# Decoder step on one core: sums of weight blocks formed by paced transfers, seven products in the down projection's middle groups, and the low-rank gate stage on quarters of the array

## The chip, the cores and the metric

One Trainium2 chip, one of its cores. The metric is the device time of one execution in microseconds. TensorE (PE) multiplies; VectorE (DVE), ScalarE (ACT) and GpSimd (POOL) work on tiles in SBUF and PSUM; SyncE (SP) here only issues transfers (DMAs). Each engine runs its own queue of instructions in order, and semaphores tie the queues together.

## The reference, cut to what matters

One layer of a decoder for 512 prompt tokens and 64 sample tokens (8 sequences of 8), 1024 channels. Weights are shared.

```
mk, mv = rmsnorm(mem) @ w_xk, rmsnorm(mem) @ w_xv
z = rmsnorm(x) @ w_in        # GLA q,k,v,r, low-rank gate (16 columns), retention q,k,v,g, two merge gates
log_alpha = log_sigmoid(ga_low @ w_gla_a2 + b) / 16        # forget gate of the GLA branch
o_g, o_r = chunked linear attention with decays, per head, with states
merged = sigmoid(gate_a) * norm(o_g) * silu(gr) + sigmoid(gate_b) * norm(o_r) * silu(rg)
x = x + rmsnorm(merged @ w_mix_out)
x = x + rmsnorm(cross_attention(rmsnorm(x)))               # 4 heads, 256 memory tokens
x = x + rmsnorm(square(relu(rmsnorm(x) @ w_up)) @ w_down)  # 4096 hidden
```

## The kernel before

Activations lie channel by token: 576 columns, in two halves of 288 (`NH`), each half 256 prompt and 32 sample tokens. Every float32 operand of a product is split into a high and a low part (`split`, L92 to L94: ACT casts the high part, DVE subtracts to get the low part; `split_p`, L98, has POOL subtract). A product is then three matmuls, high by high, high by low, low by high (`mm3`, L251 to L253). `gemm_m` makes one output block of 128 columns: 8 steps of the inner dimension by three matmuls by two halves, 48 matmuls.

Weights come in tiles of 128 x 1024, 512 KB each, in the order of the list `plan`. `wfetch` (L180) issues the load from SP into one of six raw tiles `wraw`, `wsplit` splits it into `wh` and `wl`, `wnext` hands it to a product.

The stages: keys and values of the memory (`mem`), with the norms of x beside them (`prenorm`, L363, whose low parts `xl` POOL subtracts; `rstd`, L333, takes the power -1/2 on POOL, `dg`, L335, spreads it into a diagonal on DVE, and PE makes it a row by L342). Then the mixers: first the low-rank gate stage, then eight units, each one head of retention or of GLA. In a unit POOL computes the rotary sum (L890), the scaled keys `ks` (L1063), the power of each head's norm (L874), gates `G` (L1127) and merges (L1136). Then the output projection, cross-attention, and the MLP in four groups g of 1024 hidden channels: up, relu squared, down into the sum `y3`.

The gate stage (L806 to L809) takes a weight `w_ga` of 128 columns that holds the 16 columns three times, runs `gemm_m(xh, xl)` on it and leaves in `ga` the high, the low and again the high part, at partitions 0, 32 and 64. `decays` (L833) multiplies it for each GLA head.

`sevenfold` (L281) does the up products of g=1, 2, 3 in 2 x 2 blocks, by channel halves and token halves: seven products of 12 matmuls in place of eight. It needs four sums and differences of weight blocks, which DVE forms in `begin` (L213) from the two loaded tiles, and of activation blocks (`fsh`, `fsl`; A11, A12, A22, S1 to S4 are their names). The split sums lie in `wh`, `wl` and in `wq`. A block is one set of four such quarters of outputs; a group has four blocks. The up products of g=0 and all down products are plain; for g=3 the last norm is joined to them.

The program is written in order, and a scheduler then places each engine's instructions, so that independent work may stand earlier or later than it is written.

Of the kernel before, what the change touches and what calls it, by code (L numbers as in the profile page):

```python
# [13 lines left out]
P = 128  # L14
KT = 8
# [11 lines left out]


RING, STAY, RAW, SEVEN = 0, 1, 2, 3
# [29 lines left out]
def decoder_step(ctx, tc, xT, memT, ktc, vc, s_gla, s_ret, w_in, w_ga, w_a2, w_mix, w_xq, w_xk, w_xv, w_xo,  # L59
                 w_up, w_ups, w_down, vecs, cst, gam, y_out, mk_out, mv_out, sg_p, sr_p, sg_s, sr_s):  # L60
# [15 lines left out]
    ident, ones = idn[:, 0:128], idn[:, 128:256]  # L76
    def f32(ap):
        return ap.bitcast(F32)
# [60 lines left out]
    plan += [w_ga[:, 0]]  # L139
# [23 lines left out]
    def seven(w, b0):  # L163
        return [(w[b0 + b][:, kh], SEVEN) for b in range(4) for kh in range(2)]
# [6 lines left out]
    wq = []  # L171
    units = []

    def wfetch():
        if plan and sum(m == SEVEN for _, m in raws) < 2:
            src, mode = plan.pop(0), RING
            if isinstance(src, tuple):
                src, mode = src
            raw = wp.tile([P, 1024], F32, name="wraw", bufs=N_RAW)
            nc.sync.dma_start(out=raw if len(src.shape) == 2 else raw.rearrange("p (k n) -> p k n", n=src.shape[2]), in_=src)  # L180
            raws.append((raw, mode))

    def wsplit():
        if units:
            units.pop(0)()
        elif raws:
            if raws[0][1] == SEVEN:
                begin()
                return
# [4 lines left out]
            pool = staying[-1] if mode == STAY else wp  # L194
            wh = pool.tile([P, 1024], F32R, name="wh")
            wl = pool.tile([P, 1024], F32R, name="wl")
            split(wh, wl, raw)
            ready.append((wh, wl))

    def halves(w):  # L200
        return w.rearrange("p (q n) -> p q n", q=2)

    def begin():


        while len(raws) < 2:
            wfetch()
        p0, p1 = (raws.pop(0)[0] for _ in range(2))
        t = wp.tile([P, 1024], F32, name="wraw", bufs=N_RAW)
        q0, q1, qt = halves(p0), halves(p1), halves(t)  # L210

        def minus(out, a, b):
            nc.vector.tensor_tensor(out=out, in0=a, in1=b, op=ALU.subtract)  # L213

        def ring(raw):
            wh = wp.tile([P, 1024], F32R, name="wh")
            wl = wp.tile([P, 1024], F32R, name="wl")
            split(wh, wl, raw)
            ready.append((wh, wl))

        def own(raw, o, n):
            w = wq[0][:, o:o + n], wq[0][:, o + n:o + 2 * n]
            split(*w, raw)
            ready.append(w)

        def unit_a():
            ring(p0)
            wfetch()

        units.extend([unit_a, lambda: ring(t), lambda: own(p1, 0, 1024),  # L230
                      lambda: minus(q1[:, 0], q1[:, 0], qt[:, 0]), lambda: own(q1[:, 0], 2048, 512)])
        minus(qt[:, 1], q1[:, 1], q0[:, 1])
        minus(q0[:, 1], q0[:, 1], q0[:, 0])
        minus(qt[:, 0], q1[:, 1], q0[:, 1])
        wfetch()

    def wnext(n=P):

        while sum(len(r) == 2 for r in ready) < 2 and (raws or plan):
            while not units and plan and len(raws) + sum(len(r) == 1 for r in ready) < N_RAW - 1:  # L240
                n0 = len(raws)
                wfetch()
                if len(raws) == n0:
                    break
            if not raws and not units:
# [25 lines left out]


    def sevenfold(x, p1, p5, u2, c11, c22, c12, c21):


# [9 lines left out]
        def more():  # L285
            if units:
# [1135 lines left out]
```

## Time and profile before

| | us |
|---|---|
| median of three runs (lowest, highest) | 1200.71 (1199.32, 1202.62) |
| profiled execution | 1199.37 |
| its span | 1197.6 |
| PE busy in the span | 1168.7 |
| DVE busy | 746.6 |
| ACT busy | 563.3 |
| POOL busy | 155.1 |

A row of the timeline gives start, duration, engine, line, operation, the tile written and the tiles read, and in brackets how long the engine stood idle before it and what ended that. Matmuls overlap in the pipeline: one of 288 columns is listed with about 0.3 us while the next starts 0.13 us later. The memory's keys and values take the span to about 67 us, the gate stage follows, then the mixers; the up products of g=1 lie from 892 to 937 us, its down products from there to 988.

### The profile page before, as it was taken

The numbers are of one execution on the slowest core, as the hardware profiler recorded it, in microseconds if no ns is written. First come the engines' busy times: TensorE is split into PE (matmuls) and PEld (weight loads), VectorE is DVE, ScalarE is ACT, GpSimd is POOL, SyncE is SP. The second block draws the span as 40 slices with busy tenths as digits, with TensorE's granted clock in tenths as the row PEclk, the third lists the DMA queues.
The fourth block names the chain that finished last, engine by engine and source line by source line (L and its number), as shares of the span: only waits on it lengthen the run. The fifth ranks groups of instructions, "written<-read, shape, count | busy, mean of one in ns | idle before, by whom it ended". The sixth has DMA issues, their size and how long they took to land.

```text
span 1197.6 us, 21977 instructions
## 1 busy us (share of the span) xinstructions
PE 1168.7 (98%) x9006; PEld 1137.6 (95%) x9006; DVE 746.6 (62%) x1332; ACT 563.3 (47%) x992; POOL 155.1 (13%) x165
## 2 busy tenths in 40 slices
PE   8899999999999999999999999999999999999995
PEld 8899999999999999999999878989999999999995
DVE  6745757465747565757868545686937546456565
ACT  5534546442445244524555434566527416515652
POOL 0522213122312222221001000000000000000000
PEclk9899999999999999999999999999999999999998
DMA  8772424242324332322644677753223223321631
GB/s 290 228 244 79 129 79 128 72 144 72 127 89 128 89 128 79 121 88 93 213 134 138 215 260 232 235 177 123 88 71 107 88 71 105 107 71 57 215 110 60
DMA packets 65621, 158.37 MB, mean 132 GB/s; under 512 B 5648, under 2 KB 34448, under 8 KB 65392
## 3 DMA queue, kind: packets, MB, share of 16 engines
q1 hardware_dynamic: 65520, 156.96, 41.0%
q8 instruction: 71, 1.16, 0.4%
q14 instruction: 30, 0.25, 0.1%
HBM read 140.68 MB, written 16.25 MB: 131 GB/s over the span
## 4 chain that ended last, share of the span: by engine, by line
PE 90%; DVE 4%; DMA 3%; issue 1%; POOL 1%; ACT 1%; SPq 0%; POOLq 0%; DVEq 0%; ACTq 0%
PE psg L251 22%; PE psg L252 22%; PE psg L253 22%; PE psa L281 6%; PE psg L281 3%; PE psa L251 2%; PE pso L281 2%; PE psa L252 1%; PE psa L253 1%; PE pso L1241 1%; DMA xf<-in_xT 1%; PE psa L1084 1%; DVE wl L94 1%; PE pso L1079 1%; DVE res L526 1%
## 5 line engine op out<-in xcount | busy, mean ns | idle before, releaser
L251 PE MATMUL psg<-xh,wh 128*128 128x288 f32 x1296 | 385.5, 298 | 0.0
L252 PE MATMUL psg<-xh,wl 128*128 128x288 f32 x1296 | 381.9, 295 | 0.8 <-DVE wl L94 0.8
L253 PE MATMUL psg<-xl,wh 128*128 128x288 f32 x1296 | 381.9, 295 | 0.0
L94 DVE TENSOR_TENSOR wl<-wraw,wh 128x1024 fp32r<-128x1024 f32 x197 | 243.4, 1236 | 89.3 <-ACT wh L93 88.5
L93 ACT CAST wh<-wraw 128x1024 fp32r<-128x1024 f32 x197 | 207.0, 1051 | 187.6 <-PE psg L253 108.2
L251 PEld LDWEIGHTS psg<-xh,wh 128*128 128x128 f32 x1296 | 243.2, 188 | 2.2 <-issue 0.8
L252 PEld LDWEIGHTS psg<-xh,wl 128*128 128x128 f32 x1296 | 243.3, 188 | 1.1 <-DVE wl L94 1.0
L253 PEld LDWEIGHTS psg<-xl,wh 128*128 128x128 f32 x1296 | 243.1, 188 | 0.1
L251 PE MATMUL psg<-hh,wh 128*128 128x288 f32 x512 | 151.2, 296 | 0.7 <-DVE y L760 0.6
L252 PE MATMUL psg<-hh,wl 128*128 128x288 f32 x512 | 151.0, 295 | 0.3 <-DVE wl L94 0.3
L253 PE MATMUL psg<-hl,wh 128*128 128x288 f32 x512 | 151.0, 295 | 0.0
L251 PEld LDWEIGHTS psg<-hh,wh 128*128 128x128 f32 x512 | 96.2, 188 | 1.6 <-issue 1.1
L252 PEld LDWEIGHTS psg<-hh,wl 128*128 128x128 f32 x512 | 96.1, 188 | 0.6 <-DVE wl L94 0.6
L253 PEld LDWEIGHTS psg<-hl,wh 128*128 128x128 f32 x512 | 96.2, 188 | 0.0
L333 POOL TENSOR_TENSOR rs<-ms,mhalf 96x3 f32<-96x3 f32 (+1 forms) x11 | 11.0, 998 | 521.5 <-DVE ms L326 521.5
L942 ACT COPY vt<-psg 128x512 f32<-128x512 f32 x16 | 9.4, 586 | 77.8 <-PE psg L253 77.8
L874 POOL TENSOR_TENSOR rs<-mv,mhalf 128x1 f32<-128x1 f32 x48 | 29.7, 619 | 112.7 <-DVE mv L869 64.6
L944 DVE COPY vd<-psg 128x128 f32<-128x128 f32 x32 | 7.8, 285 | 55.8 <-ACT vt L942 55.8
L251 PE MATMUL psg<-bh,wh 128*128 128x288 f32 x128 | 38.4, 300 | 1.6 <-ACT wh L93 1.1
L654 DVE TENSOR_TENSOR y<-psg,y 128x576 f32<-128x576 f32 x16 | 12.1, 756 | 44.2 <-PE psg L253 44.2
L252 PE MATMUL psg<-fh,wl 128*128 128x288 f32 x128 | 38.2, 298 | 0.9 <-DVE wl L94 0.9
L253 PE MATMUL psg<-fl,wh 128*128 128x288 f32 x128 | 37.9, 296 | 0.6 <-DVE fl L94 0.6
(324 smaller groups left out, 2406.2 us busy)
## 6 DMA issues: line engine op xcount, KB each, us to landing
wraw<-in_w_in SPq DMA_DIRECT2D x64, 512.0 KB, 3.7
wraw<-in_w_down SPq DMA_DIRECT2D x38, 512.0 KB, 3.7
wraw<-in_w_ups SPq DMA_DIRECT2D x24, 512.0 KB, 3.6
wraw<-in_ktc SPq DMA_DIRECT2D x16, 512.0 KB, 5.0
wraw<-in_vc SPq DMA_DIRECT2D x16, 512.0 KB, 4.4
wraw<-in_w_xq SPq DMA_DIRECT2D x14, 512.0 KB, 3.9
wraw<-in_w_xo SPq DMA_DIRECT2D x14, 512.0 KB, 5.5
wraw<-in_w_up SPq DMA_DIRECT2D x14, 512.0 KB, 4.3
```

The source lines that it names most:

```text
L93: nc.scalar.copy(hi, src)
L94: nc.vector.tensor_tensor(out=lo, in0=src, in1=f32(hi), op=ALU.subtract)
L251: nc.tensor.matmul(out, ah, bh, start=first, stop=False)
L252: nc.tensor.matmul(out, al, bh, start=False, stop=False)
L253: nc.tensor.matmul(out, ah, bl, start=False, stop=last)
L281: nc.tensor.matmul(out, s[:, q, k], m[:, k], start=first and k == i == 0, stop=k == 3 and i == 2, skip_group_check=True)
L526: nc.vector.tensor_tensor(out=res[:, kk, c], in0=y[:, kk], in1=rj, op=ALU.add)
L654: nc.vector.tensor_tensor(out=out, in0=a, in1=b, op=op)
L874: nc.gpsimd.tensor_tensor(out=rs[:t], in0=mv[:t], in1=mhalf[:t, 0:1], op=ALU.pow)
L1079: nc.tensor.matmul(so[32 * j:32 * j + 8, o], qsd[:, b * 8:b * 8 + 8], s0[:, j], start=False, stop=True, skip_group_check=True, tile_positi ...
L1084: nc.tensor.matmul(U[:, j * 256:(j + 1) * 256], kst[g][:, 2 * bp + j, :], vst[g], start=True, stop=True)
L1241: nc.tensor.matmul(acc[rows, :256], x(h), w[:, h], start=first, stop=last, skip_group_check=True, tile_position=(0, 32 * h))
```

## The change

It does four things.

Sums of weight blocks. The blocks come as one input `w_sev`. The sums T1 = B11 + B12, T2[0] = T1 + B22, T2[1] = B12 + B22 and T4 = T2[0] + B21 are formed in a DRAM tensor `t_sev` by transfers that POOL issues (`sums`, L198 of the changed file): for each of ten groups eight of 512 KB, four that copy and four that add to what is there. `sums` is called four times in a mixer unit; where transfers are due, it has POOL copy one column of a tile of the unit (`pace`) before them. `begin`, its subtractions and the tile `wq` go.

Loads. A block of `sevenfold` loads seven pieces of 128 x 512 (256 KB), two to a raw tile, the seventh alone (`LAST`, with `wh` and `wl` of half size), where it loaded two tiles of 512 KB.

The down products of g=1 and g=2 use `sevenfold` too, so the relu squared of the up products must leave blocks and sums: `pairs` makes four sums and two splits, `ha` holds A11 and A12, a quarter of `fh` that is no longer read holds A22. The order of the seven products changes, with signs to suit.

The gate stage keeps `w_ga` as 16 columns padded to 32, unsplit, and multiplies in float32 with four inner steps at a time, one in each column quarter of the array; DVE adds the four quarters, and copies make the three parts of `ga`.

```diff
@@ decoder_step @@
+    wga = perm.tile([P, KT, 32], F32, name="wga")
...
-    plan += [w_ga[:, 0]]
...
+    def seven(b0):
+        out = []
+        for n in range(b0, b0 + 4):
+            g, i = n // 2, n % 2
+            b = [w_sev[q, n] for q in range(4)]
+            t1, t2, t4 = t_sev[g]
+            out += [((b[0], t1[i]), RING), ((t2[0, i], t2[1, i]), RING), ((b[2], b[3]), RING), ((t4[i],), LAST)]
+        return out
...
     for g in range(1, 4):
-        plan += seven(w_ups, 4 * (g - 1))
-        plan += whole(w_down, 4 * g) + (rest(whole(w_down, 12), 0) if g == 3 else [])
+        plan += seven(8 * (g - 1))
+        plan += seven(8 * g - 4) if g < 3 else whole(w_down, 4) + rest(whole(w_down, 4), 0)
+    steps = {}
+    for g, at in enumerate(SUMS_AT):
+        b11, b12, b21, b22 = (w_sev[q, 2 * g:2 * g + 2] for q in range(4))
+        t1, t2, t4 = t_sev[g]
+        for n, (dst, src, plus) in zip(SUM_STEPS, (
+                (t1, b11, 0), (t2[1], b12, 0), (t1, b12, 1), (t2[1], b22, 1),
+                (t2[0], t1, 0), (t2[0], b22, 1), (t4, t2[0], 0), (t4, b21, 1))):
+            steps.setdefault(at + n, []).append((dst, src, plus))
...
+    def sums(after):
+        if clock[0] in steps:
+            nc.gpsimd.tensor_copy(pace, after)
+        for dst, src, plus in steps.pop(clock[0], ()):
+            nc.gpsimd.dma_start(out=dst, in_=src, max_dma_last_dim=8192, **({"accum_op": ALU.add} if plus else {}))
+        clock[0] += 1
...
@@ the MLP @@
-            wq.append(biga.tile([P, 4608], F32R, name="wq", tag="biga"))
...
-        if g < 3:
             for k in range(KT):
-                ps = gemm_m(quarters(hh, hl), None)
...
+    def pairs(c1, c2, sh, sl):
+        add(c2[:, 1], c2[:, 0], c2[:, 1], ALU.subtract)
+        add(c2[:, 0], c1[:, 0], c2[:, 0], ALU.subtract)
+        split(sh[:, 2:4], sl[:, 2:4], c2)
+        add(c1[:, 0], c2[:, 1], c1[:, 0], ALU.subtract)
+        add(c1[:, 1], c1[:, 1], c1[:, 0])
+        split(sh[:, 0:2], sl[:, 0:2], c1)
...
+        for b in range(4):
+            c1, c2 = (hp.tile([P, 2, NH], F32, name="hr") for _ in range(2))
+            y = [y3[:, 2 * b:2 * b + 2, hc(half)] for half in range(2)]
...
+            sevenfold(xh7, c1, c2, lambda: add(y[0], y[0], c1), lambda: None, done21, b == 0)
@@ mixers @@
-        ps = gemm_m(xh, xl)
-        nc.scalar.copy(h2(ga), ps[:96])
-        nc.vector.tensor_tensor(out=h2(ga)[32:64], in0=ps[32:64], in1=f32(h2(ga)[32:64]), op=ALU.subtract)
+        ps = gtile()[:, :, :NH]
+        for half in range(2):
+            for i in range(4):
+                for j in range(4):
+                    k = 2 * j + i % 2
+                    nc.tensor.matmul(ps[32 * j:32 * j + 32, half], e.wga[:, k], f32((xh, xl)[i // 2][:, k, e.hc(half)]),
+                                     start=i == 0, stop=i == 3, skip_group_check=True, tile_position=(0, 32 * j))
+        gs = u2.tile([32, NT], F32, name="t1")
+        nc.scalar.copy(h2(gs), ps[0:32])
+        for j in range(1, 4):
+            nc.vector.tensor_tensor(out=h2(gs), in0=ps[32 * j:32 * j + 32], in1=h2(gs), op=ALU.add)
+        nc.scalar.copy(ga[0:32], gs)
+        nc.vector.tensor_tensor(out=ga[32:64], in0=gs, in1=f32(ga[0:32]), op=ALU.subtract)
+        nc.scalar.copy(ga[64:96], gs)
```

How the built queues move, at three places. First POOL's queue from the memory norm's power to the second half's low parts, before (`rs` is a norm's power, `xl` a low part of the normed x, `spad` a tile of the mixers):

```order
L333 TENSOR_TENSOR rs<-ms,mhalf 128x2
L333 TENSOR_TENSOR rs<-ms,mhalf 96x3
L98 TENSOR_TENSOR xl<-xn,xh 128x288 x8
L333 TENSOR_TENSOR rs<-ms,mhalf 96x3
L98 TENSOR_TENSOR xl<-xn,xh 128x288 x8
L814 MEMSET spad_897 128x128
```

The same stretch of POOL's queue after, its head; the rows with `t_sev` are the sums' transfers:

```order
L198 DMA t_sev<-in_w_sev 64x2048 x4
L198 DMA t_sev<-t_sev 64x2048
L198 DMA t_sev<-in_w_sev 64x2048
L333 ISA
L333 TENSOR_TENSOR rs<-ms,mhalf 128x2
L198 DMA t_sev<-in_w_sev 64x2048
L333 TENSOR_TENSOR rs<-ms,mhalf 96x3
L198 DMA t_sev<-in_w_sev 64x2048
L198 DMA t_sev<-t_sev 64x2048
L102 TENSOR_TENSOR xl<-xn,xh 128x288 x2
L198 DMA t_sev<-in_w_sev 64x2048
```

Six transfers stand ahead of the first `rs`, and eight more among the rest of the first half's operations (thirteen by the second half's `rs`, eighteen by the last `xl`, 32 by the first pace copy).

Second, DVE's queue at the start, around the memory norm's `ms`, before (`ss` is a sum of squares of x, `mst` a part of the memory's keys on its way out):

```order
L326 TENSOR_SCALAR ms<-psa 128x2
L335 TENSOR_TENSOR dg<-idn,rs 128x256
L397 COPY mrs<-rs 128x2
L94 TENSOR_TENSOR wl<-wraw,wh 128x1024
L353 TENSOR_TENSOR ss<-ss,sq 128x576
L415 TENSOR_TENSOR mst<-psg,mbc 128x512 x2
```

And after:

```order
L326 TENSOR_SCALAR ms<-psa 128x2
L98 TENSOR_TENSOR wl<-wraw,wh 128x1024
L353 TENSOR_TENSOR ss<-ss,sq 128x576 x2
L98 TENSOR_TENSOR wl<-wraw,wh 128x1024
L353 TENSOR_TENSOR ss<-ss,sq 128x576
L322 TENSOR_TENSOR ss<-ss 128x288
L335 TENSOR_TENSOR dg<-idn,rs 128x256
L398 COPY mrs<-rs 128x2
L326 TENSOR_SCALAR ms<-psa 96x3
L416 TENSOR_TENSOR mst<-psg,mbc 128x512 x2
```

The memory norm's `dg` moved behind two weight splits and x's sums; x's own `ms` (96x3) moved ahead of `mst`.

Third, ACT's queue at the border of the up and the down products of g=1, before (`hr` is a block of hidden values, `hh` its high part):

```order
L718 ACTIVATE hr<-hr 128x576
L723 ACTIVATE hr<-hr 128x576
L93 CAST hh<-hr 128x2x288 x2
L93 CAST wh<-wraw 128x1024
L93 CAST wq<-wraw 128x1024
L93 CAST wh<-wraw 128x1024
L93 CAST wq<-wraw 128x512
L93 CAST wh<-wraw 128x1024 x6
```

And after:

```order
L729 ACTIVATE hr<-hr 128x288
L97 CAST ha<-hr 128x2x288
L97 CAST wh<-wraw 128x512
L97 CAST hh<-hr 128x2x288
L291 COPY hr<-psa 128x288
L295 COPY hr<-psg 128x288
L97 CAST wh<-wraw 128x1024
L97 CAST hh<-hr 128x2x288
```

The copies out of PSUM for the first down block (L291, L295: c1 and c2) now stand between the splits of the last up block.

## Rows read from the trace of the kernel before

**Rows 1.** The page: the span, busy time by engine, and the chain's shares by engine

```profile
span 1197.6 us, 21977 instructions
...
PE 1168.7 (98%) x9006; PEld 1137.6 (95%) x9006; DVE 746.6 (62%) x1332; ACT 563.3 (47%) x992; POOL 155.1 (13%) x165
...
PE 90%; DVE 4%; DMA 3%; issue 1%; POOL 1%; ACT 1%; SPq 0%; POOLq 0%; DVEq 0%; ACTq 0%
```

**Rows 2.** Windows: length, PE, PEld, DVE, ACT, POOL busy; clock; DMA share, GB/s

```profile
10.00:20.00 10.00, 9.66 (x71) 9.46 (x71) 8.58 (x14) 7.15 (x11) 0.70 (x1) 0.87 1.05 408
40.00:50.00 10.00, 6.95 (x50) 6.54 (x49) 8.72 (x10) 5.74 (x10) 5.79 (x5) 0.84 0.92 282
76.00:300.00 224.00, 223.25 (x1741) 219.45 (x1739) 136.42 (x307) 100.13 (x197) 49.56 (x52) 1.00 0.34 107
892.00:937.00 45.00, 45.00 (x338) 44.76 (x336) 29.68 (x39) 30.06 (x51) 0.00 (x0) 1.00 0.37 117
937.00:988.00 51.00, 51.00 (x385) 50.86 (x384) 23.97 (x28) 11.55 (x15) 0.00 (x0) 1.00 0.20 63
```

**Rows 3.** Waits of PE: for whom, us in total, times, longest

```profile
PE psa L324 <- DVE ss L322: 3.0, 1, 3.0
...
PE psa L342 <- DVE dg L335: 2.7, 4, 1.7
```

**Rows 4.** The chain that ended last, in order: start, us, what, records

```profile
657.90 1.00 PE pso L1241 x16
...
891.81 1.60 PE psa L281 x12
...
935.29 1.60 PE psa L281 x12
...
988.05 1.60 PE psa L281 x12
```

**Rows 5.** Groups, 890 to 940 us: count | busy us, mean ns | idle before, releaser

```profile
L93 ACT CAST wh<-wraw 128x1024 fp32r<-128x1024 f32 x9 | 9.5, 1054 | 10.8 <-PE psa L281 10.8
...
L93 ACT CAST hh<-hr 128x576 fp32r<-128x576 f32 x8 | 4.9, 668 | 0.0
...
L726 ACT COPY hr<-psa 128x288 f32<-128x288 f32 x4 | 1.6, 395 | 0.0
```

**Rows 6.** The page: transfers of the mixers' weights over the whole span

```profile
wraw<-in_w_in SPq DMA_DIRECT2D x64, 512.0 KB, 3.7
```

**Rows 7.** Timeline of PE, the gate stage's first matmul (start us, us)

```profile
67.56 0.30 PE L251 MATMUL psg<-xh,wh 128*128 128x288 f32 x1
```

**Rows 8.** One line of PE: ns min/median/max, first and last start, shapes

```profile
L833 PE MATMUL psg<-ga,a2s x8: 294/338/383, 136.9 to 448.2; 96*128 96x288 f32 x8
```

**Rows 9.** Timeline of SP: one issue

```profile
15.49 0.33 SPq L180 DMA_DIRECT2D wraw<-in_w_xv  x1
```

**Rows 10.** Timeline of POOL

```profile
19.30 0.70 POOL L333 TENSOR_TENSOR rs<-ms,mhalf 128x2 f32<-128x2 f32 x1 [18.79 <-DVE ms L326]
...
64.56 1.44 POOL L98 TENSOR_TENSOR xl<-xn,xh 128x288 fp32r<-128x288 f32 x1 [0.32 <-ACT xh L97]
...
292.77 1.04 POOL L1063 TENSOR_TENSOR ks<-klo,cm 128x512 fp32r<-128x512 f32 x1 [13.32 <-DVE klo L1040]
```

**Rows 11.** Transfers of 0 to 76 us: totals; one group, KB each, us to landing

```profile
DMA packets 9465, 20.07 MB, mean 264 GB/s; under 512 B 925, under 2 KB 5149, under 8 KB 9459
...
wraw<-in_w_xk SPq DMA_DIRECT2D x8, 512.0 KB, 7.6
```

**Rows 12.** Timeline of DVE at the start

```profile
20.03 0.43 DVE L335 TENSOR_TENSOR dg<-idn,rs 128x256 f32<-128x256 f32 x1 [0.82 <-POOL rs L333]
...
27.07 0.46 DVE L322 TENSOR_TENSOR ss<-ss 128x288 f32<-128x288 f32 x1
```

**Rows 13.** One line of DVE: ns min/median/max, first and last start

```profile
L909 DVE COPY qf<-t x4: 427/428/428, 87.8 to 521.8; 128x512 f32<-128x512 f32 x4
```

More of the change, by code (lines that the diff above doesn't have):

```diff
@@ L170, in decoder_step @@
+    clock = [0]
+    pace = perm.tile([P, 1], F32, name="pace")
+    def sums(after):
[4 more added lines that the diff above has]
+        clock[0] += 1
     raws, ready, staying = [], [], []
-    wq = []
-    units = []
+    wdp = []
     def wfetch():
-        if plan and sum(m == SEVEN for _, m in raws) < 2:
+        if plan:
@@ L193, in wsplit, with wmore @@
                 return
[L194 to L197, printed above, removed]
+            n = 512 if mode == LAST else 1024
+            pool = wdp[0] if mode == LAST else staying[-1] if mode == STAY else wp
+            wh = pool.tile([P, n], F32R, name="wh")
+            wl = pool.tile([P, n], F32R, name="wl")
+            split(wh, wl, raw[:, :n])
             ready.append((wh, wl))
[L200 to L206, printed above, removed]
+    def wmore():
+        while plan and len(raws) < N_RAW - 1:
             wfetch()
[L208 to L235, printed above, removed]
+        wsplit()
     def wnext(n=P):
         while sum(len(r) == 2 for r in ready) < 2 and (raws or plan):
-            while not units and plan and len(raws) + sum(len(r) == 1 for r in ready) < N_RAW - 1:
-                n0 = len(raws)
+            while plan and len(raws) + sum(len(r) == 1 for r in ready) < N_RAW - 1:
                 wfetch()
-                if len(raws) == n0:
-                    break
-            if not raws and not units:
+            if not raws:
                 break
@@ L381, in decoder_step @@
         nc.sync.dma_start(out=idn, in_=cst[:, C_ID:C_ID + 256])
+        nc.sync.dma_start(out=wga, in_=w_ga)
         wsplit()
@@ L683, in decoder_step, with xh7 @@
         hl = acta.tile([P, 4, 4, NH], F32R, name="hl", tag="xl")
+        plain = g in (0, 3)
+        ha = None if plain else biga.tile([P, 2, 2, 4, NH], F32R, name="ha", tag="biga")
+        def xh7(n):
+            if n in SQ:
+                return hh[:, SQ[n]], hl[:, SQ[n]]
+            return (fh[:, 2], fl[:, 2]) if n == "A22" else (ha[:, 0, n == "A12"], ha[:, 1, n == "A12"])
         if g == 0:
@@ L739, in decoder_step, with done21 @@
+        if plain:
+            break
+        for b in range(4):
+            c1, c2 = (hp.tile([P, 2, NH], F32, name="hr") for _ in range(2))
+            y = [y3[:, 2 * b:2 * b + 2, hc(half)] for half in range(2)]
+            def done21(ps):
+                nc.scalar.copy(c2[:, 0], ps)
+                add(y[1], y[1], c2)
+            sevenfold(xh7, c1, c2, lambda: add(y[0], y[0], c1), lambda: None, done21, b == 0)
     res2 = fsp.tile([P, KT, NT], F32, name="res2", tag="fsh")
@@ L1122, in unit @@
                 tick()
+            sums(G[:, 1, NT - 1:])
             for m in range(2):
@@ L1128, in unit @@
                 tick()
+            sums(G[:, 1, NT - 1:])
             def finish():
```

159 lines of the change are left out of this document (79 added, 80 removed).

## The prediction

> **What bounds the kernel now.** I read the page first: its span, the busy shares and the chain of waits [rows 1]. TensorE (PE) is busy for 98% of the span and carries 90% of the chain, so time leaves this kernel in two ways: fewer matmuls, or less of what interrupts them. Next come the windows by stage [rows 2]. In the MLP (892 to 988 us) and in the first mixers (76 to 300 us) PE has hardly a gap, and its granted clock is 1.00, the level of 2.4 GHz. The start is different: from 40 to 50 us PE is busy for 6.95 of 10 us, and from 10 to 20 us the transfers fill their engines (share 1.05 at 408 GB/s). The waits of PE [rows 3] tell what it lacks there: VectorE (DVE) steps of the norms. So a matmul saved in the MLP counts in full as long as the others keep up, and work added at the start can cost time at once.
>
> **The down products: seven in place of eight.** The chain's pieces in the MLP [rows 4] show one of the seven products of an up block: 12 matmuls in 1.60 us, 0.133 us each. Four blocks of seven are 336 matmuls. The up group of g=1 takes 936.9 - 891.8 = 45.1 us: from the start of its first product to the end of its last (935.29 + 1.60). The down group behind it, eight plain products of 48, takes 988.05 - 936.9 = 51.2 us. The changed down group has the up group's form. It therefore loses 48 matmuls, by the rows 51.2 - 45.1 = 6.1 us (by the product 48 x 0.133 = 6.4), and two such groups lose **12.2 us**. PE has no gap in either window [rows 2], so all of it lies on the path, if the others can feed it.
>
> Can they? In a middle up block (g=1, 2) the order gives ScalarE (ACT) 17 instructions where it had 13 (30.06 us in four blocks, 7.5 each [rows 2]); the four more are smaller splits and copies. By the means of wh, hh and copies [rows 5] the 17 come to 10.45 us, against 11.3 us for a block (45.1 / 4). They overlap a little at their ends, as the 13 do, so I take 8.8. Placed in order, the copy that PE needs first (c1 from A11's bank) is ready 0.8 us before it is asked for. DVE stays near 7.4 us of 11.3: it loses the weights' subtractions and gets the activations' sums. What is late first is thus ACT, by 0.8 us of room, and not here.
>
> At the border of up and down, PE needs the last block's A11 and A12 operands. The order puts the first three blocks' matmuls ahead, and the last block's relu, square and splits run beside them. I count 0 to 0.5 us for each of four borders; **+0.5** in all.
>
> **The weights' loads there.** Each seven-block now loads seven pieces of 256 KB, 1.75 MB where it was 1 MB, so 7 MB in 45 us, 155 GB/s. The window shows 117 GB/s at a share of 0.37 [rows 2] and the start 408, so this costs nothing. The loads of a block land in 3.7 us in the middle of the kernel [rows 6], and one block takes 11.3.
>
> **The gate stage.** Before, it is 48 matmuls of 288 columns at 0.133 us (the first starts at 67.56 [rows 7]): 6.4 us. Now it is 32 fp32 matmuls, each on a quarter of the array. The attention's L1241 has this form, four quarters in turn with 256 columns: 16 records, which are eight fp32 matmuls of two passes each, in 1.00 us [rows 4]. A group of four takes 0.50 us, at 288 columns 0.56, and eight groups 4.5 us: **-1.9 us**. If the quarters did not overlap here, each matmul would cost what a group does, 18 us, that is +11.6. Nothing speaks for that, since L1241 alternates its quarters as the new loop does. The three adds and copies behind it sit ahead of the first use of `ga`, at 136.9 us [rows 8], some 60 us later; they are covered.
>
> **The sums' transfers: what they are held by.** Eighty transfers of 512 KB, 42 MB, are issued from GpSimd (POOL). The diff paces them with copies; the built order shows how little these hold. Of the 80, 32 stand ahead of the first pace copy, and 18 ahead of the last `xl` of the prenorms. They are held by each other: in one of the ten groups six transfers follow in series (copy T1, add, copy T2, add, copy T4, add), and each waits on POOL's queue for the landing of the one before. Whatever stands behind that wait on POOL waits too: the norms' pow `rs`, the low parts `xl` and `ql`, the retention's `ks`, the pow of each head's norm, the merges.
>
> *Landing, in the mixers.* The 80 stand between 0 and about 280 us of the times before, with two groups in flight: 10 x 6 / 2 = 30 steps in 280 us, 9.3 us for a step. A step takes issue and landing. I bound the issue on POOL, which no row shows, by SyncE's issue of 0.33 us [rows 9] and by a POOL operation over a whole tile, 1.44 us [rows 10]; I take 0.7, what POOL's smallest pow takes [rows 10]. I bound the landing from below by SyncE's transfers of the same size, 3.7 us [rows 6], and from above by twice the 7.6 us of the crowded start [rows 11], since an added sum reads its target and writes it. I take 6 for the mixers, where the transfers' share is only 0.34 [rows 2]: nearer to the low row. A step is then 6.7 us against 9.3, and POOL runs ahead. Walking down POOL's built order with the times before as earliest starts, I find no operation over 1.5 us late after the start. With 42 MB more, the share in 76 to 300 us rises from 0.34 to about 0.7, and single weight loads come later; six buffers of raw weights cover some of it. I put **+1 us** on the mixers (0 to 3).
>
> *At the start.* Six transfers stand ahead of POOL's first `rs` (19.30 us [rows 10]). They move 3.1 MB, at 408 GB/s 7.7 us of all the engines' time, while these are full. By 66 us eighteen have been issued, 9.4 MB, and with the 20.07 MB of 0 to 76 us [rows 11] that is 29.5 MB, 72 us at 408 GB/s: all that there is. Loads of x and of the memory's weights come later by up to 7.7 us, less where the transfers pause (from about 21 to 25 us). Against that stands what PE can spare: the last `xl` ends at 66.00 [rows 10] and PE takes it at 67.56 [rows 7], and PE loses 3.0 and 1.7 us there already [rows 3], which a new delay partly replaces. DVE's order shows such a replacement: the memory norm's `dg`, which follows `ms` at once before (20.03 [rows 12]), stands behind two weight splits, three sums of squares and x's last sum (27.07 in the times before [rows 12]). PE needs it for the third block of keys; I make that a stall of about 5.5 us near 25 us, and the stalls of 3.0 and 1.7 us, which came from the same chain of x, go. With landings of 8 us the walk makes `xl` 3.5 us late, of which 1.5 are spare. In all I take **+4 us** for the start: 2 for `xl` and 2 for loads. Its bounds are 0 (the wait for `dg` just takes the place of the old ones) and 10 (the loads' 7.7 and more of the lateness).
>
> The Trainium skill, "SBUF — State Buffer", section Summary: rules for kernel authors, speaks against issuing transfers from GpSimd: DVE in its faster modes starves the writing of their descriptors. DVE's copy L909, 0.43 us for 512 elements [rows 13], is the kind of operation that it means, and none here holds its engine longer than that by much. If each issue waited out one or two of these, it would take 1.2 us, a step 7.2, and the walk would give up to 3 us in all, within the bounds above; no trace of before shows such an issue. "DMA: Bandwidth & Descriptors", section SWDGE (gpsimd) path, gives 2.0 us plus the bytes at 436 GB/s for a transfer, by which an estimate for 524,288 bytes is 3.2 us, under the lower bound that I take from rows.
>
> **Sum.** The profiled execution took 1199.37 us, 1.3 under the median of 1200.71. 1199.37 - 12.2 - 1.9 + 0.5 + 4 + 1 = 1190.8; on the median **1192 us**.
>
> **The rivals.**
> *The transfers hold POOL's queue (slower).* The point is 9.3 us a step. One microsecond beyond it is 30 steps late at the end, some 30 us in POOL's order, and PE waits for `ks` and the norms of that unit. With 10.4 us a step (landing 9.7) the walk puts the `ks` of 292.77 us [rows 10] 19 us late. PE has its next unit's products to fill 3 to 5 us of that, so 14 to 15 us are lost: 1192 + 14 = 1206. For it: an added sum moves its bytes more often, and a start landing is 7.6 already. Against: the engines are a third busy in the mixers.
> *The start is not repaid (no change).* The x loads come 7.7 us later and nothing of it hides, or `dg`, the loads and `xl` cost one behind the other: +9 to +10 where I have 4, so 1197 to 1199.
> *ACT becomes the bound in the eight middle up blocks.* If the 17 instructions did not overlap and waited for PE's banks too, a block would grow by 0.9 us; 8 x 0.9 = 7 gives 1199. Against: 10.45 us by full means is still under 11.3.
> *It gives more.* The stalls at the start only change place and the mixers lose nothing: 1192 - 5 = 1187, or with shorter borders 1185.
>
> **How the numbers follow.** My forecast (1187 to 1196) has 0.55, the better case 0.07, the two that end near no change 0.18, the held queue 0.20. A measurement of this kernel tells about 0.3%, 3.6 us, from no change: faster is under 1197.1, slower over 1204.3. Faster: 0.62; same 0.18; slower 0.20. The range runs from 1185, the sum with the start and the mixers at their lower bounds, to 1206, the held queue at its first price; a held queue beyond that is left out. For the forecast alone it is 1187 to 1196.
>
> **What would show it.** Right: down groups of g=1 and g=2 at 45 to 46 us each; the gate stage at 4.5 us with 64 short records; POOL's transfers landing in 5 to 8 us, with the 80th before 300 us; a wait of PE for `dg` near 25 us; PE at the gate by 70 to 72 us. Wrong: transfers that land in over 9 us, POOL operations waiting for transfers in mixer units 2 and 3, and PE waiting for `ks` or `rs`; up blocks of 12 us with PE waiting for ACT; PE at the gate after 76 us.

## The result: slower by 0.7%

The changed kernel took 1210.26 us (median of four runs, 1206.02 to 1211.94), the kernel before 1200.77 beside it: a ratio of 1.007, interval 1.0054 to 1.0086. The forecast was 1192, range 1185 to 1206: the kernel got slower where a gain was forecast. The profiled execution has a span of 1208.6 us, 11.0 more than before.

The page: span, busy time, queues of the transfers (packets, MB, share of 16 engines over the span; q0 is what POOL issues, q1 what SP issues), and the chain by engine.

```profile
span 1208.6 us, 22379 instructions
...
PE 1163.6 (96%) x8926; PEld 1128.7 (93%) x8926; DVE 763.1 (63%) x1374; ACT 596.3 (49%) x1069; POOL 210.7 (17%) x274
...
q1 hardware_dynamic: 79920, 172.30, 43.6%
q0 software_dynamic: 6400, 41.95, 14.1%
...
PE 84%; DMA 7%; DVE 5%; ACT 1%; issue 1%; POOL 1%; SPq 0%; POOLq 0%; DVEq 0%; ACTq 0%
```

PE is busy for 5.1 us less than in [rows 1], so work was saved; but the span grew, so PE stands idle for some 16 us more. In the chain the transfers have 7% where they had 3%. Where the time went is read from five places that both traces have:

| PE (or POOL) at | before | after | later by |
|---|---|---|---|
| gate stage's first matmul | 67.56 | 79.04 | 11.5 |
| first scaled keys `ks` | 104.99 | 123.13 | 18.1 |
| thirteenth `ks` | 479.9 | 500.9 | 21.0 |
| first product of g=1 | 891.7 | 914.9 | 23.2 |
| first down product of g=3 | 1129.2 | 1140.1 | 10.9 |

From the first product of g=1 on the MLP gained 12.3 us, as forecast. Everything before it lost 23.2. The windows show both (length, PE, PEld, DVE, ACT, POOL busy, granted clock, DMA share, GB/s):

```profile
10.00:20.00 10.00, 8.81 (x48) 8.30 (x48) 5.80 (x11) 5.81 (x12) 1.83 (x3) 0.69 1.04 309
40.00:50.00 10.00, 10.00 (x70) 9.89 (x70) 4.89 (x8) 5.55 (x9) 2.05 (x3) 0.82 0.98 310
76.00:300.00 224.00, 215.89 (x1681) 208.60 (x1681) 130.84 (x288) 97.40 (x188) 89.95 (x123) 0.98 0.92 256
915.00:960.00 45.00, 45.00 (x340) 45.00 (x339) 33.92 (x52) 34.24 (x63) 0.00 (x0) 1.00 0.48 147
960.00:1005.00 45.00, 45.00 (x335) 44.46 (x335) 29.99 (x43) 23.30 (x38) 0.00 (x0) 1.00 0.52 164
```

From 10 to 20 us PE issued 48 matmuls where it had 71 [rows 2]; from 76 to 300 us 1681 where it had 1741, with the transfers' share at 0.92 instead of 0.34. In the two windows of the MLP PE has no gap and the clock is whole.

The first 76 us as a whole, before and after:

```profile
0.00:76.00 76.00, 68.33 (x490) 65.94 (x491) 47.46 (x68) 40.31 (x66) 23.61 (x23) 0.93 0.80 264
0.00:76.00 76.00, 59.94 (x402) 57.59 (x403) 45.44 (x63) 36.62 (x59) 27.72 (x37) 0.87 0.99 329
```

Before, PE has no gap from its gate stage to 76 us, after, none from 70 us to its gate stage, so up to the gate it stands idle for 7.7 us before and 16.1 after: 8.4 of the 11.5 us are waits. In the other 3.1 PE is busy longer with the same work, at a lower granted clock (0.87 instead of 0.93).

The chain in the MLP gives the down group of g=1 (start us, us, records):

```profile
958.24 2.80 PE psa L277 x21
...
1003.69 3.20 PE psa L277 x24
```

The first piece holds the last 12 up matmuls and nine of the first down product, the second the last down product and the first of g=2. So the down products run from 958.24 + 1.60 = 959.84 to 1003.69 + 1.60 = 1005.29: 45.4 us, where eight plain products took 51.2 [rows 4].

The transfers' issues over the whole span (KB each, median us from issue to landing) show what the start suffers from:

```profile
wraw<-in_w_in SPq DMA_DIRECT2D x64, 512.0 KB, 5.2
t_sev<-in_w_sev POOLq DMA_DIRECT2D x60, 512.0 KB, 8.1
...
wraw<-in_w_xk SPq DMA_DIRECT2D x8, 512.0 KB, 11.2
wraw<-in_w_xv SPq DMA_DIRECT2D x8, 512.0 KB, 9.8
...
xf<-in_xT SPq DMA_DIRECT2D x8, 288.0 KB, 11.5
```

The memory's weights land in 11.2 us where they took 7.6 [rows 11]. PE's waits (total, times, longest) follow:

```profile
PE psa L342 <- DVE dg L335: 7.9, 4, 4.8
PE psg L247 <- DVE t L839: 5.8, 1, 5.8
PE psg L247 <- ACT mh L387: 4.6, 1, 4.6
```

Of the wait for `dg` 5.9 us lie before the gate: 4.8 at 30.8 us, and 1.1 in x's second half. The wait for `t` is one that the prediction had not listed. The timelines of the engines behind the gate stage tell its story (start us, us, engine, operation, in brackets idle time and what ended it):

```profile
82.37 0.84 ACT L448 ACTIVATE mst<-psg,mrs 128x256 f32<-128x256 f32 x2 [1.50 <-DMA out_mv<-mst]
83.22 0.63 ACT L837 COPY t<-psg 32x576 f32<-32x576 f32 x1
83.23 0.55 SPq L449 DMA_DIRECT2D out_mv<-mst  x1
83.88 0.75 DVE L839 TENSOR_TENSOR t<-psg,t 32x576 f32<-32x576 f32 x1 [2.16 <-ACT t L837]
...
92.63 0.33 SPq L816 DMA_DIRECT2D cm<-in_cst  x1
92.65 0.62 ACT L825 CAST a2s<-t 96x512 fp32r<-96x512 f32 x1 [8.80 <-DMA out_mv<-mst]
93.30 0.68 DVE L826 TENSOR_TENSOR a2s<-t,a2s 32x512 fp32r<-32x512 f32 x1 [8.67 <-ACT a2s L825]
94.02 1.54 DVE L839 TENSOR_TENSOR t<-psg,t 32x576 f32<-32x576 f32 x2
...
95.70 0.58 PE L247 MATMUL psg<-xh,wh 128*128 128x288 f32 x1 [5.82 <-DVE t L839]
```

The tiles of the mixers (`a2s`, the table `cm`) lie where the memory stage's tiles lay, and must wait until its last output `out_mv` has left. It was issued at 83.23, behind an ACT step that itself waited for an earlier `out_mv`, and landed at 92.5; before, the last one was issued at 69.5 and landed at 75.9. DVE's queue has the subtraction for `a2s` between the three adds that empty the gate's PSUM bank, so the bank stays taken until 95.6, and PE, which has filled the next bank by 89.9, stands. Its clock then falls to 0.50, the level of 1.2 GHz:

```profile
96.00:100.00 4.00, 4.00 (x18) 4.00 (x18) 0.75 (x1) 1.98 (x3) 0.00 (x0) 0.50 1.00 389
100.00:104.00 4.00, 4.00 (x27) 4.00 (x27) 3.49 (x4) 0.00 (x0) 2.05 (x2) 0.81 0.99 164
```

Those 8 us hold 45 matmuls; at 0.133 us there would be 60, so 2.0 us are lost beside the 5.8.

### The profile page after: what moved, and what is told of

The parts are those of the page before. It is cut to its first block, busy times and chain, and to the rows that moved or that the text cites. A ratio compares the mean times of both kernels' runs of the same rounds, so it can differ in the third digit from the quotient of the medians.

```text
span 1208.6 us, 22379 instructions
## 1 busy us (share of the span) xinstructions
PE 1163.6 (96%) x8926; PEld 1128.7 (93%) x8926; DVE 763.1 (63%) x1374; ACT 596.3 (49%) x1069; POOL 210.7 (17%) x274
## 3 DMA queue, kind: packets, MB, share of 16 engines
q0 software_dynamic: 6400, 41.95, 14.1%
## 4 chain that ended last, share of the span: by engine, by line
PE 84%; DMA 7%; DVE 5%; ACT 1%; issue 1%; POOL 1%; SPq 0%; POOLq 0%; DVEq 0%; ACTq 0%
PE psg L247 18%; PE psg L249 18%; PE psg L248 18%; PE psa L277 11%; PE psg L277 5%; PE pso L277 3%; DMA xf<-in_xT 2%; DMA out_mv<-mst 2%; PE psa L247 1%; DVE wl L98 1%; PE psa L248 1%; PE psa L249 1%; DMA out_sgs<-sn 1%; PE pso L1278 1%; DMA wraw<-in_w_xo 1%
## 5 line engine op out<-in xcount | busy, mean ns | idle before, releaser
L98 DVE TENSOR_TENSOR wl<-wraw,wh 128x1024 fp32r<-128x1024 f32 (+1 forms) x236 | 284.8, 1207 | 118.6 <-ACT wh L97 112.8
L97 ACT CAST wh<-wraw 128x1024 fp32r<-128x1024 f32 (+1 forms) x236 | 239.1, 1014 | 145.9 <-PE psg L249 55.2
L247 PE MATMUL psg<-hh,wh 128*128 128x288 f32 x256 | 76.0, 297 | 0.7 <-DVE y L781 0.6
L248 PE MATMUL psg<-hh,wl 128*128 128x288 f32 x256 | 75.5, 295 | 0.3 <-DVE wl L98 0.3
L249 PE MATMUL psg<-hl,wh 128*128 128x288 f32 x256 | 75.4, 295 | 0.0
L198 POOL DMA_DIRECT2D t_sev<-in_w_sev x60 | 45.5, 803 | 40.0 <-DMA t_sev<-t_sev 26.8
L247 PEld LDWEIGHTS psg<-hh,wh 128*128 128x128 f32 x256 | 48.1, 188 | 1.2 <-issue 1.1
L248 PEld LDWEIGHTS psg<-hh,wl 128*128 128x128 f32 x256 | 48.0, 188 | 0.6 <-DVE wl L98 0.6
L249 PEld LDWEIGHTS psg<-hl,wh 128*128 128x128 f32 x256 | 48.0, 188 | 0.2 <-DVE hl L98 0.2
```

The costliest lines, as they stand in the source:

```text
L97: nc.scalar.copy(hi, src)
L98: nc.vector.tensor_tensor(out=lo, in0=src, in1=f32(hi), op=ALU.subtract)
L198: nc.gpsimd.dma_start(out=dst, in_=src, max_dma_last_dim=8192, **({"accum_op": ALU.add} if plus else {}))
L247: nc.tensor.matmul(out, ah, bh, start=first, stop=False)
L248: nc.tensor.matmul(out, al, bh, start=False, stop=False)
L249: nc.tensor.matmul(out, ah, bl, start=False, stop=last)
```

## The experiments

All ratios are to the kernel before, run beside each on the same chip; its median there was 1200.8 to 1202.8 us. "Gate" and "13th ks" are times in the profiled execution, which is not always a middling one: e4's took 1203.96 us, 5 over its median, e13's 1192.51, 3 under.

| run | median us | ratio (interval) | gate | 13th ks |
|---|---|---|---|---|
| before | 1200.77 | 1 | 67.6 | 479.9 |
| after | 1210.26 | 1.007 (1.0054 to 1.0086) | 79.0 | 500.9 |
| e1 no sums | 1187.17 | 0.9873 (0.984 to 0.9905) | 65.2 | 476.2 |
| e2 paced | 1194.56 | 0.9942 (0.9922 to 0.9962) | 67.9 | 484.1 |
| e3 gate only | 1199.60 | 0.9981 (0.9963 to 1.0) | 66.8 | 478.2 |
| e4 copies | 1198.85 | 0.998 (0.9965 to 0.9996) | 75.9 | 493.3 |
| e5 behind start | 1191.28 | 0.9919 (0.9894 to 0.9945) | 66.8 | 480.6 |
| e6 a2 early | 1216.75 | 1.0125 (1.01 to 1.015) | 80.5 | 503.3 |
| e7 POOL time | 1188.16 | 0.989 (0.9867 to 0.9913) | 66.0 | 479.6 |
| e8 half later | 1193.60 | 0.9932 (0.9908 to 0.9955) | 65.8 | 479.5 |
| e9 few bytes | 1330.49 | 1.1064 (1.1029 to 1.11) | 74.5 | 577.3 |
| e10 consts early | 1213.90 | 1.0093 (1.0063 to 1.0123) | 77.1 | 501.5 |
| e11 bytes only | 1208.53 | 1.0083 (1.0052 to 1.0114) | 78.6 | 499.7 |
| e12 dg early | 1212.85 | 1.0104 (1.0078 to 1.013) | 82.0 | 501.4 |
| e13 order only | 1195.85 | 0.9958 (0.9939 to 0.9977) | 69.9 | 484.4 |

### Without the transfers, and with them held back

e1 takes the transfers out of `sums` (the loads take raw blocks in place of the sums):

```diff
-        for dst, src, plus in steps.pop(clock[0], ()):
-            nc.gpsimd.dma_start(out=dst, in_=src, max_dma_last_dim=8192, **({"accum_op": ALU.add} if plus else {}))
         clock[0] += 1
```

e2 queues each step behind its pace copy (`issue_after` fixes the order on POOL, with no wait of its own); e5 queues all of them behind the first pace copy (`first[0]` in the place of `held.ins`) and leaves them free after it; e8 is e2 with other times, and with calls of `sums` in the MLP of g=0 to g=2:

```diff
-SUMS_AT = (2, 5, 7, 10, 12, 15, 17, 20, 22, 25)
+SUMS_AT = (2, 6, 11, 16, 21, 26, 32, 42, 52, 62)
...
-            nc.gpsimd.tensor_copy(pace, after)
+            held = nc.gpsimd.tensor_copy(pace, after)
         for dst, src, plus in steps.pop(clock[0], ()):
+          with tc.issue_after(held.ins):
```

> The changed kernel without the 80 transfers that form the sums: the loads of the seven-blocks take raw blocks of the same size in their place, so the up and down products of g=1 to 3 are not the reference's. Theory A (the transfers that stand at the head of POOL's queue crowd the start, and with them out PE comes to the gate stage at about 67 us instead of 79.0 and does not wait 5.8 us behind it): 1185 to 1189 us, that is 12.3 us for the seven products and 2.4 for the gate stage under the kernel before. Theory B (the gate stage's new form makes the wait of 5.8 us behind it, whatever the transfers do): 1190 to 1195, with the wait still there. Theory C (the seven-blocks' smaller loads or ACT cost time in the MLP): above 1195.

> The changed kernel with one addition: each step's transfers are queued on POOL behind their pace copy, so that none can stand at the start; the first goes out in the first mixer unit, the last before 540 us. Theory A (crowded start): the start is that of the kernel before, PE at the gate at 67 to 69 us, 1186 to 1191 us. Rival (the 42 MB cost in the mixers too, by late weight loads and by POOL's issues): the start is repaid but the mixers grow by 5 us or more, 1193 to 1200.

> The changed kernel with all 80 transfers queued behind the first pace copy (about 118 us) and not paced after it. If the start alone made the loss: PE at the gate at 65 to 68 us and the time within 2 us of the paced version (1194.6). If holding POOL's queue in the mixers is dear too (norms and scaled keys behind waits for landings of 8 us): 1198 to 1206 us.

> The paced version with the sums of six groups spread over all eight mixer units (48 transfers instead of 80) and those of four groups put into the MLP of g=0 and g=1, where POOL has no other work; they are not needed before 1027 us. If the mixers' loss goes with the transfers in them: 1190 to 1193 us. If the MLP then waits for its weight loads (7 MB a group beside the sums): 1194 or more.

e1 measured 1187.2: the other three parts of the change are worth 1.3%, and the transfers cost all of that and 0.7% more, some 23 us. The wait of 5.8 us is not among e1's waits, so the gate's form does not make it. With the transfers held out of the start, 16 to 19 us of the 23 come back, and e5 (1191.3) and e2 (1194.6) beat both kernels. e2 came out in its rival's case; e5 is 3.3 us under e2, outside both of its cases, with its gate where the first one has it. Both are over e1, by 4 and 7 us, and so is e8 (1193.6, by 6), which came out between its two cases: with fewer transfers in the mixers and more in the MLP the loss is about the same. The window from 76 to 300 us in e5 is

```profile
76.00:300.00 224.00, 221.72 (x1719) 216.88 (x1717) 134.00 (x307) 99.69 (x197) 89.52 (x117) 1.00 0.81 227
```

and PE issues 1719 matmuls there; e1, at a share of 0.34, issues 1737. Pacing within the mixers gained nothing over e5; the intervals of e2, e5 and e8 overlap.

### The gate stage alone

The edit is the last part of the change's diff, from `ps = gemm_m(xh, xl)` on, with its weight:

```diff
-    plan += [w_ga[:, 0]]
...
+        nc.sync.dma_start(out=wga, in_=w_ga)
...
-        ps = gemm_m(xh, xl)
+        ps = gtile()[:, :, :NH]
+        for half in range(2):
+            for i in range(4):
+                for j in range(4):
...
```

> The kernel before with only the gate stage changed (32 matmuls on quarters of the array, its small weight loaded once). Theory A: the stage takes 3.9 us instead of 6.4 and nothing waits behind it, 1197.5 to 1199.5 us. Theory B (the adds behind it hold the PSUM bank until the mixers' first tiles are free): PE waits behind it by some 3 to 6 us, 1200 to 1205.

1199.6, a ratio of 0.9981: 2.3 us less, at the edge of what can be told, and the expected size. PE waits for `t` for 0.6 us only. In the changed kernel the stage ran from 79.04 to 82.9, 3.9 us instead of 6.4.

### Bytes, adding, or POOL's time

The lines of e4 (no adding), of e7 (e1 with a fill on POOL for each transfer) and of e9 (16 of 128 rows of each), in this order:

```diff
-            nc.gpsimd.dma_start(out=dst, in_=src, max_dma_last_dim=8192, **({"accum_op": ALU.add} if plus else {}))
+            nc.gpsimd.dma_start(out=dst, in_=src, max_dma_last_dim=8192)
...
+          with tc.issue_after(held.ins):
+            nc.gpsimd.memset(idle, 0.0)
...
+            nc.gpsimd.dma_start(out=dst[..., :16, :], in_=src[..., :16, :], max_dma_last_dim=8192, **({"accum_op": ALU.add} if plus else {}))
```

> The changed kernel with the 40 adding transfers turned into plain copies of the same size (so the sums are wrong, the places in the queue the same). If the start is crowded by bytes moved, whatever is done to them: 1206 to 1211 us, like the changed kernel, with landings of about 8 us. If it is the adding that is dear: landings of the changed 40 fall by a third or more, and the time to 1196 to 1203.

> The kernel without the transfers (1187.2 us), with a fill of 832 columns on POOL (about 0.8 us, what an issue took) in the place of each of the 80, behind the pace copies. The products of g=1 to 3 work on raw blocks, as there. If the paced version's 7 us over 1187 are POOL's time: 1191 to 1195. If they are the bytes (later weight loads, share 0.72 instead of 0.34 in the mixers): 1186 to 1189.

> The changed kernel with each of the 80 transfers cut to an eighth (64 KB, 16 of 128 rows), unpaced and at the head of POOL's queue as there; the seven-blocks load raw blocks, so the products of g=1 to 3 are not the reference's. If the loss is the bytes that crowd the loads at the start: PE at the gate at 65 to 69 us and 1187 to 1191 us, beside 1187.2 without any transfer. If it is POOL's queue (issues, and norms behind waits for landings) or DVE's changed order (the memory norm's dg behind x's sums): PE at the gate after 72 us and 1195 us or more.

e4 has all five queues (PE, DVE, ACT, POOL and SP) with the same operations in the changed kernel's own order, so it is a clean test of the adding: 1198.9, 11 us less, in the middle of its second case. POOL's queue and its transfers there:

```profile
q0 software_dynamic: 6400, 41.95, 10.2%
...
t_sev<-in_w_sev POOLq DMA_DIRECT2D x60, 512.0 KB, 5.9
```

The same bytes take 10.2% of the 16 engines' span instead of 14.1%. That is 0.141 x 1208.6 = 170 us against 0.102 x 1202.3 = 123: 1.5 us of all engines for a copy, and 1.2 more for one that adds. So half of the loss goes with the adding, most likely by the engines' time that it takes: the only other thing seen to change is POOL's issue (median 0.52 us instead of 0.78), and e7 below bounds that. The other half is there with plain copies.

e7 measured 1188.2: POOL's own time for 80 issues costs about a microsecond over e1. The fills do not imitate another thing, POOL standing still until a transfer has landed: 59 us in all in the changed kernel, 52 in e5, 6 in e2. But e2, where it hardly stands, loses no less than e5. So what the two lose in the mixers goes most likely with the bytes; no run moves the bytes without POOL.

e9 failed as an experiment. With 64 KB each the transfers were placed otherwise, and the scheduler ordered every engine's queue anew: 1330 us, with PE waiting in all mixer units. Its gate, at 74.5 us, lies in the second case, with a wait of 9.4 us for `dg`: in that order PE comes 9 us later than in e1 with hardly any bytes. A transfer's shape changes the order of engines that never touch it, so a run with other sizes does not tell bytes from order.

### The wait behind the gate

e6 moves one tile, e10 the pool of the mixers' constants, which it opens before the memory stage:

```diff
-        a2s = c1.tile([96, 512], F32R, name="a2s")
+        a2s = e.perm.tile([96, 512], F32R, name="a2s")
...
+    c1 = c1s.enter_context(tc.tile_pool(name="mxc", bufs=1))
     with tc.tile_pool(name="mem", bufs=1) as mp:
```

> The changed kernel with the gate's second weight tile (a2s) in memory that no earlier stage uses, so that its cast waits only for its own load (landed at 50 us) and not for the memory values' last output. Theory: the 5.8 us that PE waits behind the gate stage, for the PSUM bank which DVE frees behind the a2s subtraction, and the 2 us of half clock that follow, go: 1200 to 1204 us, with the start as late as in the changed kernel. If the bank is held by something else: 1208 to 1212.

> The changed kernel with the mixers' constants (the table cm of 1.6 MB, a2s, ga, spad) in a pool that is opened before the memory stage, so that their loads and first uses do not wait until the memory values' last output has landed (92.5 us). Transfers as in the changed kernel. If the 9 us that PE loses between the gate stage and the first unit's scaled keys come from that wait (moving a2s alone only moved the wait to cm): the waits of 5.8 us for t and the half clock go, 1200 to 1204 us. If the table's 1.6 MB, now loaded in the crowded start, delays PE as much there: 1206 to 1212.

Both misses: 1216.8 and 1213.9. e10 is no better than the changed kernel, and e6 is worse, clear of the intervals. Rows of e6 (PE's waits; DVE's timeline), then of e10 (PE's waits; ACT's timeline):

```profile
PE psg L247 <- DVE t L922: 5.8, 1, 5.8
...
100.82 0.76 DVE L919 TENSOR_TENSOR t<-psg,cm 128x576 f32<-128x576 f32 x1 [6.12 <-DMA cm<-in_cst]
```

```profile
PE psg L247 <- DVE t L842: 7.5, 1, 7.5
...
94.11 0.63 ACT L840 COPY t<-psg 32x576 f32<-32x576 f32 x1 [11.01 <-DMA out_mv<-mst]
```

In e6 the gate's bank is free in time, and the wait of 5.8 us comes one product later, where DVE needs the table `cm`, whose load waits for the same output. In e10 `cm` is early, and the gate's own work tile now lies over the memory stage. The wait belongs to whatever tile is laid there. It is gone where the output lands early, in e1, e2 and e5 (0.3 us or less; in e7, without transfers too, 1.7 are left). In e6 and e10 the stretch from the 13th `ks` to the MLP is also 4 to 5 us longer than in the changed kernel; no run shows why.

### Order or bytes at the start

e1, e2 and e5 take the transfers out of the start and give DVE, and with it the other queues, the old order there back, both at once. Three runs part them.

e13 is e5 with the memory norm's `dg` (`made[0]`) tied behind x's last sum of squares, as the changed kernel has it. e12 is the changed kernel with DVE's later work of the keys tied behind that `dg`. e11 is e5 and 18 plain copies of 512 KB from POOL into unused memory, none waiting for another's data: six at the head and one behind each of the first twelve `xl`. Their lines, in this order:

```diff
+            if len(made) == 1:
+                tc.add_manual_dep(made[0], total.name, mybir.DependencyInfo(mybir.DependencyClass.NoSync, mybir.DependencyReason.DATA), reason="late")
...
+                    behind = ExitStack()
+                    behind.enter_context(tc.issue_after(made[0]))
...
+        spare.append(nc.gpsimd.dma_start(out=t_x[n], in_=w_sev[n % 4, 2 * (n // 4):2 * (n // 4) + 2], max_dma_last_dim=8192))
...
+    for n in range(6):
+        crowd()
...
+            with tc.issue_after(held.ins):
+                crowd()
```

> The version with all transfers behind the first pace copy (1191.3 us), and DVE's order at the start made that of the changed kernel: the memory norm's dg behind two more weight splits, three sums of squares and x's last sum. No transfer of the sums runs before 115 us. If the order makes the start late: PE waits some 5 us for dg and is at the gate at 70 us or later, 1194 to 1198 us. If the old stalls only change place, or the bytes are the cause: gate at 66 to 69 us, 1190 to 1193.

> The changed kernel, transfers as there, with DVE's order at the start mended: all that DVE does for the memory keys after the first block stands behind the memory norm's dg, so that dg follows ms after one sum of squares. If the order makes the start late: the wait for dg of 4.8 us goes and the gate comes 4 to 6 us earlier than 79.0, 1203 to 1207 us. If the bytes make it: the gate within 2 us of 79.0 and 1208 to 1212.

> The version with all transfers behind the first pace copy (1191.3 us), and 18 plain copies of 512 KB from POOL into unused memory in the start: six at the head of its queue, one behind each of the first twelve xl. They add up to the changed kernel's eighteen, without its adding and without its waits between them. If the bytes make the loss: loads of x and of the memory's weights land in 10 us or more, PE at the gate after 73 us, 1197 us or more. If it is the waits of the transfers for each other on POOL's queue: gate at 66 to 69 us, 1190 to 1193.

e13, as its first case has it: the order alone makes one wait of 4.6 us for `dg` and costs 3.1 us at the gate, 4.6 in the median (the two intervals overlap by 0.0006). PE's waits there:

```profile
PE psa L349 <- DVE dg L342: 6.5, 3, 4.6
```

e12: mending the order under the transfers gains nothing, 1212.9, with the gate at 82.0, later than either case has it. The wait for `dg` shrinks from 4.8 to 2.7, and one of 4.3 for `ss` takes its place:

```profile
PE psg L247 <- DVE t L844: 6.3, 1, 6.3
PE psa L344 <- DVE dg L337: 5.7, 4, 2.7
PE psg L247 <- ACT mh L389: 5.1, 1, 5.1
...
PE psa L324 <- DVE ss L322: 4.3, 1, 4.3
```

e11: the bytes, without adding and without waits between them, bring the loss back: 1208.5 where e5 has 1191.3, the gate at 78.6. By 76 us fourteen of its eighteen copies have been issued, six of them in the first 5 us; in the changed kernel seventeen, the sixth at 17.6. Its landings and first waits:

```profile
wraw<-in_w_xk SPq DMA_DIRECT2D x8, 512.0 KB, 10.2
```

```profile
PE psg L262 <- ACT mh L402: 9.5, 3, 5.0
PE psa L357 <- DVE dg L350: 6.5, 3, 4.6
PE psg L262 <- DVE t L854: 3.3, 1, 3.3
```

The wait for `mh` is for the memory itself, which all engines' transfers delay; that for `dg` shows that e11's DVE order is the late one too, so of its 17 us some 5 are put down to order, by e13. The rest is most likely contention, the transfers' bytes against the loads of the first 40 us, but e11's order differs in more than that `dg` (the one of x's second half comes at 74.7 us, in e13 at 53.6), so that share is argued and not measured. That the transfers wait for each other on POOL's queue is not needed for it.

## Why the prediction was wrong

**Right: the products.** Two down groups, 12.2 us forecast, 12.3 measured between the first product of g=1 and the down products of g=3; each group 45.4 us. The borders cost nothing where 0.5 was allowed. ACT did not become the bound: 34.24 us in the up window, 8.6 of 11.3 a block. **Right: the gate**, 2.5 us instead of 1.9. **Right: the pacing does not hold**, as read from the order. **Right: the rival that POOL's queue is held by landings over 9.3 us a step did not come**: issue 0.8 and landing 7.7 (medians) stay under it. The 80th transfer landed at 315 us where the prediction named 300 as a sign, with all of the mixers some 20 us late.

**Wrong: the term for the start**, +4 with bounds 0 to 10. Up to the gate it measured 11.5, outside the bounds. The step that failed is how the bytes were priced. The sum divided by 408 GB/s, the rate of one stretch of 10 us: 29.5 MB in 72 of the first 76 us, "all that there is"; and then it took 2 us for the loads. (Of the eighteen transfers that it counted by 66 us, fourteen had been issued.) Over the whole 76 us the kernel before moved 264 GB/s at a share of 0.80, which is 330 for a full share, so its own 20 MB held the engines for 60.5 us and left 15.5. With the sums in, the queues moved 25.03 MB in that time, at a share of 0.99: 329 GB/s with every engine full. SP's queue before, then totals and queues after:

```profile
q1 hardware_dynamic: 9459, 19.99, 79.2%
```

```profile
DMA packets 9530, 25.03 MB, mean 329 GB/s; under 512 B 1062, under 2 KB 4853, under 8 KB 8565
...
q1 hardware_dynamic: 8325, 17.10, 62.1%
q0 software_dynamic: 1200, 7.87, 36.7%
```

SP's own loads got 17.10 MB through where they had 19.99. The 7.87 MB of sums took 0.367 x 76 = 27.9 us of all engines, 3.5 us a MB against 2.8 for SP's (0.621 x 76 / 17.1): half of the 80 transfers add, and no row of before showed what adding takes. When the engines are full, that time is added to somebody's load; it should have stood in the sum at 28 us less the 15.5 that were idle, some 12: an estimate made afterwards, and close to the 11.5. Made the same way for e4 it gives 8 us (0.309 x 76 - 15.5), and e4's gate came 8.3 later than before. For e11 it gives 4 (0.257 x 76 - 15.5), and its gate came 11.8 later than e5's: when the transfers go out, and the order that comes with them, count too.

**Missing: what the late start triggers.** Nothing in the sum stood between the gate and the first unit; there 9.1 us net of the gate's own gain were lost (18.1 - 11.5 + 2.5), of which the wait of 5.8 and the slow clock's 2.0 are seen above. In the kernel before the table's load was issued at 76.45, early enough to be hidden. The prediction followed queues and engines, and not which memory a tile inherits and whose transfer must have left it.

**Mis-sized: the mixers**, +1 with bounds 0 to 3, measured 2.9 by the thirteenth `ks`. The same price is behind it: a share of about 0.7 was forecast for 76 to 300 us, and 0.92 measured. 0.7 us more were lost by the MLP, and 1.5 in the MLP's first group, whose first 24 us ran at a granted clock of 0.93. Those 1.5 do not go with the sums at the start and count as chance: they stand in the profiles of e5, e6, e10 and e12 too, and not in those of e1, e2, e4, e11 and e13.

By these steps: 11.5 - 2.5 + 9.1 + 2.9 + 0.7 + 1.5 - 12.3 = 10.9 us, which is the measured 11.0.

**The stall for dg** was named (about 5.5 us near 25 us; 4.8 at 30.8 us, and 4.6 in e13 alone). That it would only replace old stalls was the error, and in part a misread row: the waits of [rows 3] are those of the whole span. At the start the waits for `dg` were 0.7 us in two:

```profile
PE psa L342 <- DVE dg L335: 0.7, 2, 0.6
```

The 1.7 us is at the last norm, at 1187 us, and it is there in the changed kernel too (1198 us). So only the 3.0 for `ss` could go; it went in the changed kernel, and 1.6 of it were left in e13.

**POOL's issues.** The median issue on POOL is 0.78 us in the changed kernel and 0.52 in e4, where all queues, DVE's among them, have the same order: the difference goes with the adding. e7 shows that 80 times 0.8 us on POOL are worth about a microsecond. The Trainium skill ("SBUF — State Buffer", Summary: rules for kernel authors) speaks against hiding a transfer issued from GpSimd under DVE's work, since the writing of its descriptors starves while DVE is in its faster modes. No run here shows that by itself. The formula of the Trainium skill's "DMA: Bandwidth & Descriptors", section SWDGE (gpsimd) path, gives an estimate of 3.2 us for these transfers; their median landings were 8.1 us (6.9 for those that read `t_sev`) and in e4, without adding, 5.9, all in crowded engines. The measured ones decide.

What stays open: how much of the 17 us of e11 is order; why its plain copies hold the gate up as long as the sums do, while e4's, in the changed kernel's order, hold it up less (75.9); why e2 and e5 differ, if they do.

## What to carry to other kernels

Before adding background transfers, find the stretch where the engines of the transfers are already full (share near 1.0) and keep them out of it: in this kernel the same 42 MB cost 23 us when a fifth of it ran in the first 76 us, with the order that came with it, and 4 to 7 when none did. Price the bytes there by the idle share of the whole stretch and not by the rate of its best 10 us. Pacing written as code order is no pacing if a scheduler may move the transfers ahead of it; read the built order, and tie them explicitly. And when a stage gets later, look for tiles that are laid over its memory: they wait for its last store to land, and moving one tile only hands the wait to the next.

## What the runs showed of the hardware

A transfer from memory to memory that adds took 2.7 us of all 16 engines for 512 KB, a plain one 1.5 (80 took 14.1% of the span with half adding, 10.2% with none, in the same order of all queues; held out of the start, in e2, e5 and e8, the 80 with half adding took 14.2 to 15.1%). Over the first 76 us the loads alone moved 264 GB/s at a share of 0.80, loads and sums together 329 at 0.99: the same 330 for a full share, where one stretch of 10 us had shown 408. And with the transfers' engines full, a store of 256 KB took 12.1 us at the median (4.4 before), which held up the next use of its tile and the tiles laid behind it. Before, then after:

```profile
out_mv<-mst SPq DMA_DIRECT2D x4, 256.0 KB, 4.4
out_mv<-mst SPq DMA_DIRECT2D x4, 256.0 KB, 12.1
```
